# A hybrid decoder step on one core: where the last group's products stand among its slabs, and three small edits at the end of the second half

## The chip, the cores and the metric

The kernel runs on 1 core of one Trainium2 chip. The metric is the device time of one execution in microseconds, lower is better. Times of the kernel before: 1749.98, 1751.42 and 1751.07, median 1751.07. The engines are called as in the profile: PE (TensorE) multiplies matrices, DVE (VectorE), ACT (ScalarE) and POOL (GpSimd) work element by element, SP (SyncE) here only issues DMAs. ACT issues some DMAs too, and an engine that waits to issue one does nothing else meanwhile.

## The reference, cut to what matters

One layer for 256 prompt tokens and 8 x 8 sample tokens, 320 in all, with a model width of 2048. The change lies in the second half, the convolutional feed-forward network:

```python
def conv_ffn(h, conv_state, w_up, conv_w, conv_b, w_down):
    up = h @ w_up                                    # 2048 -> 2 * 5632
    up, new_conv = causal_depthwise_conv(up, conv_state, conv_w, conv_b)
    g, u = jnp.split(up, 2, axis=-1)
    return (jax.nn.gelu(g, approximate=True) * u) @ w_down, new_conv

def rms_norm(x, w):
    xf = x.astype(jnp.float32)
    y = xf * lax.rsqrt(jnp.mean(xf * xf, axis=-1, keepdims=True) + EPS)
    return (y * w.astype(jnp.float32)).astype(x.dtype)

    f, new_ffn_conv = conv_ffn(rms_norm(x, p["norm_ffn_pre"]), ffn_conv_state,
                               p["ffn_w_up"], p["ffn_conv_w"], p["ffn_conv_b"], p["ffn_w_down"])
    x = x + rms_norm(f, p["norm_ffn_post"])
```

## The kernel before

**Products in three matmuls.** Everything is float32. A weight or an activation is split into a rounded high part and a low part: for a slab of weights `wraw`, ACT casts `whi` (line 124) and DVE subtracts it to get `wlo` (line 125). A product is then three matmuls, high by high, high by low and low by high (lines 135 to 137 for the up-projection, line 1472 for the prompt tokens in the down-projection).

**Groups.** The 5632 hidden columns are cut into 11 groups of 512, numbered 0 to 10. `ffn_up(g)` makes the up-projection of a group: 16 slabs of 512 KB, 24 matmuls each, first the gate half, then the other half. DVE copies the result out of PSUM into `pad` (lines 1338, 1339), ACT and DVE do the convolution (`gcv`, `ucv`; lines 1345, 1347), ACT the GELU, and DVE multiplies into `a` and `a_s` for prompt and sample tokens (lines 1355, 1356). `cut` splits quarters of `a` into `a11`, `a12`, `a21`, `a22` (high parts on ACT, line 398, low parts on DVE, line 399).

**The down-projection one group behind.** While PE works on the slabs of group g, `down_steps` makes the down-projection of group g - 1. It does so for two halves of the output columns (m = 0, 1), each with seven products of half-sized blocks in place of eight, after Strassen and Winograd. Their weights are the four loaded blocks `b11`, `b12`, `b22`, `b21` and four combinations t1 to t4 that POOL makes from them (line 1513, each in four pieces); t3, t2 and t4 are written over the blocks b12, b11 and b21. The order of products in a half is 1 (b11), 2 (b21) with the sample tokens' products `pms` ahead of it, 5 (t1), 7 (t3), 3 (b22), 6 (t2), 4 (t4). For each, ACT and DVE split the weights (lines 1487, 1488), PE makes six matmuls into `pm`, and DVE adds `pm` to a sum (line 1466). `together(m)` then combines the seven sums of a half into blocks of the output with seven additions on DVE (line 1566).

**What sets the order.** `down_steps` is a generator. After each slab of an up-projection `tick` advances it by one step, so one product stands behind each slab. It first yields two or more times without work, and so starts that many slabs later. What is left after the last slab runs at once, without slabs between. A scheduler then orders each engine's instructions; an engine runs them in that order.

**The last group.** Group 10 has no group behind it whose slabs could hide its down-projection. `down_plain` makes it plainly, in eight steps of 256 x 512 weights (two row pairs i times four column blocks nb), called steps one to eight below. `held_w` (step two, and step four for the other row pair) and `kept` are weights that stay for a second use; step one is (nb 0, i 0), step two (nb 1, i 0), step three (nb 0, i 1), step four (nb 1, i 1), then the same for nb 2 and 3. Behind steps two, four, six and eight come the samples' products `pds`. Row pair i = 1 needs `a12` and `a22`. Tokens 128 to 255 (c = 1) are finished first, then the samples (c = 2), then tokens 0 to 127 (c = 0).

**The end.** For each finished block (c, nb), `one_block` sums the squares on ACT and multiplies the block by the norm's weights, in place; `whole(c, ...)` makes the inverse root of the mean square with a handful of one-column steps on DVE and ACT (`last_s`, `last_v`, `last_r`, `last_n`), adds the scaled blocks to `x1_tok` and stores them as y. For two blocks of c = 1 ACT scales and POOL adds (lines 1708, 1709), for the others DVE does both (line 1711).

**x1 in rows.** `to_rows`, four times in the first half of the products of group 0, turns x1 on DVE (line 1448) and stores it to memory from SP (line 1451); `load_x1` reads it again at the end as `x1_tok`.

Of the kernel before, what the change touches and what calls it, by code (L numbers as in the profile page):

```python
# [8 lines left out]
F32 = mybir.dt.float32  # L9
# [3 lines left out]
ALU = mybir.AluOpType  # L13
# [3 lines left out]
P = 128  # L17
# [16 lines left out]
def hybrid_step(  # L34
# [10 lines left out]
    act, dve, pool, pe, sp = nc.scalar, nc.vector, nc.gpsimd, nc.tensor, nc.sync  # L45
# [1261 lines left out]
    with tc.tile_pool(name="fp", bufs=1) as fp:  # L1307
# [92 lines left out]
        NG = NF // 4  # L1400
# [81 lines left out]
        def down_steps(ck, parts):  # L1482
# [9 lines left out]
            if ck == 0:  # L1492
                for _ in range(3):
                    yield
            else:
                for _ in range(5 if ck == NG - 2 else 2):
                    yield
            for m in (1, 0) if ck == 0 else (0, 1):
# [24 lines left out]
                product(1, "a11", "b11")  # L1523
                if ck == 0 and m == 1:
                    to_rows(0)
                yield
# [7 lines left out]
                if ck == 0 and m == 1:  # L1534
                    to_rows(1)
                yield
                raw["t3"] = raw["b12"]
                less(raw["t3"], "b22", "b12")
                product(5, "s1", "t1")
                yield  # L1540
                raw["t2"] = raw["b11"]
# [101 lines left out]
        gain_s = hp.tile([P, 1024], F32, tag="ohi", name="gain_s")  # L1643
        unread = hp.tile([P, 512], F32, tag="olo", name="unread")
        x1_tok = hp.tile([P, 5, 1024], F32, tag="h_lo", name="x1_tok").rearrange("p a b -> p (a b)")
# [26 lines left out]
        def one_block(c, nb):  # L1672
            t, g, _ = of(c, nb)
            by_vector = c == 0 and nb > 1
            with first() if by_vector else nullcontext():
                act.activation(unread, t, AF.Square, accum_out=squares[:, c, nb:nb + 1])
                (dve if by_vector else pool).tensor_tensor(out=t, in0=t, in1=g, op=ALU.mult)
                if c < 2 and nb == 2:
                    most[c] = fp.tile([P, 1], F32, name=f"most{c}")
                    dve.tensor_reduce(out=most[c], in_=squares[:, c, :3], axis=mybir.AxisListType.X, op=ALU.add)  # L1680
                    dve.tensor_scalar(out=most[c], in0=most[c], scalar1=1.0 / D, scalar2=EPS, op0=ALU.mult, op1=ALU.add)
# [13 lines left out]
        def whole(c, some, others):  # L1695
            with first():
# [7 lines left out]
                for nb in range(2 if c == 2 else 4):  # L1704
# [7 lines left out]
                    if c < 2:  # L1712
                        (act if by_two or c == 0 and nb % 2 else sp).dma_start(o_y[P * c:P * c + P, 512 * nb:512 * nb + 512], y)
                if c == 2:
# [96 lines left out]
```

## Time and profile before

| | |
|---|---|
| time of the profiled execution | 1750.16 us |
| its span, first to last instruction | 1748.4 us |
| median of three runs | 1751.07 us |
| PE busy | 1727.3 us, 99% |
| DVE busy | 1365.8 us, 78% |
| ACT busy | 880.1 us, 50% |
| POOL busy | 694.9 us, 40% |

A row of the timeline gives the start, the duration, the engine, the line, the operation, out<-in, the shape and a count; in brackets the idle time of the engine before it and what ended that. "<-DVE wlo L1488" means that DVE's instruction of line 1488, which writes `wlo`, ended the wait. A matmul row's duration is longer than the distance to the next one, since matmuls are pipelined; distances from start to start are the better measure.

### The profile page before, as it was taken

To read this page: it belongs to the slowest core of one execution; us is meant where nothing else is said; L and a number is where in the kernel's file an instruction comes from. 1 tells how busy PE (TensorE), PEld (TensorE's weight loads), DVE (VectorE), ACT (ScalarE), POOL (GpSimd) and SP (SyncE) were. 2 spreads that over 40 slices of the span, in tenths; PEclk is the share of its full clock that TensorE was granted. 3 is DMA by queue.
4 is the path that set the end of the run, shared out by engine and by line. 5 is a ranking of instruction groups with operands and counts; after the bars stand their busy time and mean duration, and the time that the engine had idled before them with its cause. 6 is when DMAs were issued, how large, how long until landed. Compare 5 with 4: busy or idle time off the path is not lost.

```text
span 1748.4 us, 29947 instructions
## 1 busy us (share of the span) xinstructions
PE 1727.3 (99%) x11223; PEld 1606.9 (92%) x11223; DVE 1365.8 (78%) x2133; ACT 880.1 (50%) x1274; POOL 694.9 (40%) x1003
## 2 busy tenths in 40 slices
PE   9999999999999999999999999999999999999987
PEld 9999999999999999999988888988888888888874
DVE  6559864667979787878987788879797979797897
ACT  6344544334656664645565444444444545454543
POOL 2532230000422323121355656565555556565463
PEclk9999999999999999999999999999999999999998
DMA  8776665555676776654765454454545454545353
GB/s 265 223 231 182 182 176 157 154 165 185 211 228 205 216 230 215 217 178 155 241 187 149 147 158 147 146 179 150 167 148 164 153 161 146 162 154 159 122 168 125
DMA packets 214482, 310.60 MB, mean 178 GB/s; under 512 B 22080, under 2 KB 115904, under 8 KB 214144
## 3 DMA queue, kind: packets, MB, share of 16 engines
q1 hardware_dynamic: 196800, 279.23, 52.4%
q0 software_dynamic: 6176, 13.87, 2.6%
q10 hardware_dynamic: 11360, 15.57, 2.6%
q8 instruction: 88, 1.44, 0.3%
q14 instruction: 58, 0.48, 0.1%
HBM read 285.00 MB, written 22.32 MB: 176 GB/s over the span
## 4 chain that ended last, share of the span: by engine, by line
PE 94%; DVE 3%; POOL 2%; issue 1%; ACT 0%; DVEq 0%; ACTq 0%; POOLq 0%
PE ps L135 20%; PE ps L137 20%; PE ps L136 20%; PE pm L1472 10%; PE pd L135 4%; PE pd L136 4%; PE pd L137 4%; PE pms L1479 3%; POOL b L1513 1%; PE pd L1472 1%; PE y_ps L1088 1%; PE ps_v L136 1%; PE ps_v L135 1%; PE ps_v L137 1%; DVE wlo L1488 1%
## 5 line engine op out<-in xcount | busy, mean ns | idle before, releaser
L137 PE MATMUL ps<-h_hi,wlo 128*128 128x320 f32 x2428 | 749.1, 309 | 1.4 <-DVE wlo L125 1.3
L135 PE MATMUL ps<-h_hi,whi 128*128 128x320 f32 x2428 | 750.1, 309 | 0.0
L136 PE MATMUL ps<-h_lo,whi 128*128 128x320 f32 x2428 | 748.6, 308 | 0.0
L125 DVE TENSOR_TENSOR wlo<-wraw,whi 128x1024 fp32r<-128x1024 f32 (+2 forms) x395 | 490.1, 1242 | 146.3 <-ACT whi L124 144.3
L124 ACT CAST whi<-wraw 128x1024 fp32r<-128x1024 f32 (+2 forms) x394 | 406.2, 1031 | 370.0 <-PE ps L136 142.1
L135 PEld LDWEIGHTS ps<-h_hi,whi 128*128 128x128 f32 x2428 | 455.7, 188 | 9.0 <-issue 1.3
L136 PEld LDWEIGHTS ps<-h_lo,whi 128*128 128x128 f32 x2428 | 455.8, 188 | 6.2
L137 PEld LDWEIGHTS ps<-h_hi,wlo 128*128 128x128 f32 x2428 | 455.5, 188 | 2.6 <-DVE wlo L125 2.6
L1488 DVE TENSOR_TENSOR wlo<-b,whi 128x1024 fp32r<-128x1024 f32 x120 | 154.0, 1284 | 77.2 <-ACT whi L1487 76.0
L1487 ACT CAST whi<-b 128x1024 fp32r<-128x1024 f32 x120 | 125.4, 1046 | 163.8 <-PE ps L136 147.0
L1513 POOL TENSOR_TENSOR b<-b,b 128x256 f32<-128x256 f32 x160 | 185.9, 1186 | 0.0
L135 PE MATMUL pd<-ohi,whi 128*128 128x320 f32 x448 | 138.7, 310 | 0.0
L137 PE MATMUL pd<-ohi,wlo 128*128 128x320 f32 x448 | 138.3, 309 | 0.0
L136 PE MATMUL pd<-olo,whi 128*128 128x320 f32 x448 | 138.3, 309 | 0.0
L1350 POOL COPY ptf<-pad 128x2 f32<-128x2 f32 x88 | 41.0, 465 | 177.7 <-DVE pad L1338 177.2
L1513 POOL TENSOR_TENSOR b<-b,t 128x256 f32<-128x256 f32 x80 | 78.6, 992 | 69.9 <-PE pms L1479 67.5
L1513 POOL TENSOR_TENSOR t<-b,b 128x256 f32<-128x256 f32 x80 | 90.4, 1159 | 26.6 <-DMA b<-in_ffn_w_down 26.5
L135 PEld LDWEIGHTS pd<-ohi,whi 128*128 128x128 f32 x448 | 84.1, 188 | 0.6
L136 PEld LDWEIGHTS pd<-olo,whi 128*128 128x128 f32 x448 | 84.1, 188 | 0.3
L137 PEld LDWEIGHTS pd<-ohi,wlo 128*128 128x128 f32 x448 | 84.1, 188 | 0.0
L248 DVE TENSOR_TENSOR acc_mix<-acc_mix,pd 128x320 f32<-128x320 f32 (+1 forms) x113 | 53.5, 477 | 27.6 <-PE pd L137 27.5
L1479 PE MATMUL pms<-b,a_s 128*64 128x512 f32 x320 | 74.1, 599 | 0.0
(417 smaller groups left out, 2498.2 us busy)
## 6 DMA issues: line engine op xcount, KB each, us to landing
wraw<-in_ffn_w_up SPq DMA_DIRECT2D x176, 512.0 KB, 4.6
wraw<-in_w_in SPq DMA_DIRECT2D x132, 512.0 KB, 3.8
b<-in_ffn_w_down SPq DMA_DIRECT2D x80, 512.0 KB, 4.6
wraw<-in_w_out SPq DMA_DIRECT2D x64, 512.0 KB, 3.5
st<-in_state_ssm SPq DMA_DIRECT2D x40, 256.0 KB, 4.5
out_ssm_state_sample<-st ACTq DMA_DIRECT2D x30, 256.0 KB, 2.4
cs<-dacs_d SPq DMA_DIRECT2D x16, 320.0 KB, 5.5
wraw<-in_w_in SPq DMA_DIRECT2D x12, 384.0 KB, 4.1
```

The costliest lines, as they stand in the source:

```text
L124: rounded[:] = [act.copy(hi, raw).ins]
L125: lowered[:] = [dve.tensor_tensor(out=lo, in0=raw, in1=hi.bitcast(F32), op=ALU.subtract).ins]
L135: pe.matmul(ps, whi, xhi, start=first, stop=False)
L136: pe.matmul(ps, whi, xlo, start=False, stop=False)
L137: last_made[0] = pe.matmul(ps, wlo, xhi, start=False, stop=last).ins
L248: added_last[:] = [dve.tensor_tensor(out=acc[:, nb, ts], in0=acc[:, nb, ts], in1=ps[:, ts], op=ALU.add).ins]
L1350: kept_rows[:] = [pool.tensor_copy(ptf[:, k, :], pad[:, 256:258]).ins]
L1472: last_made[0] = pe.matmul(ps, x[xi][:, k], w[wi][:, 512 * k:512 * k + 512], start=start and k + i == 0, stop=stop and k == 1 and i == 2).ins
L1479: last_made[0] = pe.matmul(ps[64 * h:64 * h + 64], a_s[:, k0 + k], w[h][:, 512 * k:512 * k + 512], start=start and k == 0, stop=stop and k ...
L1487: rounded[:] = [act.copy(hi, raw).ins]
L1488: dve.tensor_tensor(out=lo, in0=raw, in1=hi.bitcast(F32), op=ALU.subtract)
L1513: pool.tensor_tensor(out=to[:, cs], in0=raw[x][:, cs], in1=raw[y][:, cs], op=ALU.subtract)
```

## The change

Five edits in the second half:

1. For the last group that has steps (`ck == NG - 2`, group 9, whose products run among group 10's slabs) `down_steps` yields two times without work and not five.
2. Two of the stores of y for c = 1, those of the blocks that POOL adds, are issued by SP and not by ACT.
3. Block (0, 1) is multiplied by the norm's weights on DVE and not on POOL.
4. Block (0, 3), the last, is multiplied into a room of its own (`scaled_last`, the second half of the tile that held `unread`) and not in place.
5. The first two turns of x1 are called one product later each.

```diff
@@ down_steps
-                for _ in range(5 if ck == NG - 2 else 2):
+                for _ in range(2):
                     yield
@@
                 product(1, "a11", "b11")
-                if ck == 0 and m == 1:
-                    to_rows(0)
                 yield
@@
                 product(2, "a12", "b21")
                 if ck == 0 and m == 1:
-                    to_rows(1)
+                    to_rows(0)
                 yield
                 raw["t3"] = raw["b12"]
                 less(raw["t3"], "b22", "b12")
                 product(5, "s1", "t1")
+                if ck == 0 and m == 1:
+                    to_rows(1)
                 yield
@@
-        unread = hp.tile([P, 512], F32, tag="olo", name="unread")
+        spare = hp.tile([P, 2, 512], F32, tag="olo", name="unread")
+        unread, scaled_last = spare[:, 0], spare[:, 1]
@@ one_block
-            by_vector = c == 0 and nb > 1
+            by_vector = c == 0 and nb > 0
             with first() if by_vector else nullcontext():
                 act.activation(unread, t, AF.Square, accum_out=squares[:, c, nb:nb + 1])
-                (dve if by_vector else pool).tensor_tensor(out=t, in0=t, in1=g, op=ALU.mult)
+                if (c, nb) == (0, 3):
+                    f[0][3] = scaled_last
+                (dve if by_vector else pool).tensor_tensor(out=f[0][3] if (c, nb) == (0, 3) else t, in0=t, in1=g, op=ALU.mult)
@@ whole
-                        (act if by_two or c == 0 and nb % 2 else sp).dma_start(o_y[P * c:P * c + P, 512 * nb:512 * nb + 512], y)
+                        (act if c == 0 and nb % 2 else sp).dma_start(o_y[P * c:P * c + P, 512 * nb:512 * nb + 512], y)
```

What this does to the order on the engines is shown at three places. The first is ACT at the end of group 10's slabs. A cast of line 1487 belongs to a product of the seven, a cast of line 124 from `wraw` to a slab of the up-projection or to a step of the last down-projection, one from `raw` to such a step; line 398 cuts the quarters of `a`. Before:

```order
L1487 CAST whi<-t_18393 128x1024
L124 CAST whi<-wraw 128x1024
L1487 CAST whi<-b_18345 128x1024
L1487 CAST whi<-b_18347 128x1024
L398 CAST a_hi<-a 128x256
L1487 CAST whi<-b_18343 128x1024
L1345 ACTIVATE ucv<-pad,prm 128x336 x2
L1487 CAST whi<-b_18349 128x1024
L124 CAST whi<-wraw 128x1024
L124 CAST held_w<-wraw 128x1024
L124 CAST whi<-wraw 128x1024
L398 CAST a_hi<-a 128x256
```

And now, from the last two products on:

```order
L1487 CAST whi<-b_18217 128x1024
L124 CAST whi<-wraw 128x1024
L1487 CAST whi<-b_18223 128x1024
L124 CAST whi<-wraw 128x1024
L1345 ACTIVATE ucv<-pad,prm 128x336
L124 CAST held_w<-wraw 128x1024
L1345 ACTIVATE ucv<-pad,prm 128x336
L124 CAST whi<-wraw 128x1024
L124 CAST held_w<-raw 128x1024
L124 CAST whi<-raw 128x1024 x2
L398 CAST a_hi<-a 128x256 x2
```

Before, the casts for products 7, 3, 6 and 4 followed the last slab's; now only that of product 4 does, and the last two quarters `a12`, `a22` are cast behind two more casts, those from `raw` for steps five and six.

The second place is DVE at the same time, where the low parts of the weights are made. Before, from the first sum behind the last slab's convolution:

```order
L1466 TENSOR_TENSOR in_fp_10060<-in_fp_10060,pm_18556 128x512
L399 TENSOR_TENSOR a12_lo_18523<-a_17739,a12_hi_18522 128x256
L1466 TENSOR_TENSOR in_fp_10060<-in_fp_10060,pm_18568 128x512
L1488 TENSOR_TENSOR wlo_18577<-b21_18349,whi_18576 128x1024
L125 TENSOR_TENSOR wlo_18599<-wraw_18597,whi_18598 128x1024
L125 TENSOR_TENSOR held_w_18588<-wraw_18617,held_w_18588 128x1024
```

And now (the rows from the first `ucv` step to the split of step three; ahead of them stand the split of product 4, the sum of product 6, the split of step one, two pairs of `pad` copies and one addition of line 1566):

```order
L1347 SCALAR_TENSOR_TENSOR ucv_18533<-pad_18528,prm_96,ucv_18533 128x336
L1566 TENSOR_TENSOR in_fp_10060<-in_fp_10060 128x512
L1347 SCALAR_TENSOR_TENSOR ucv_18533<-pad_18528,prm_96,ucv_18533 128x336
L1347 SCALAR_TENSOR_TENSOR ucv_18558<-pad_18553,prm_96,ucv_18558 128x336
L1355 TENSOR_TENSOR a_17739<-ucv_18533,gcv_17738 128x256
L1356 TENSOR_TENSOR a_s_17740<-ucv_18533,gcv_17738 128x64
L1347 SCALAR_TENSOR_TENSOR ucv_18558<-pad_18553,prm_96,ucv_18558 128x336
L1466 TENSOR_TENSOR in_fp_10060<-in_fp_10060,pm_18578 128x512
L1355 TENSOR_TENSOR a_17739<-ucv_18558,gcv_17738 128x256
L1356 TENSOR_TENSOR a_s_17740<-ucv_18558,gcv_17738 128x64
L125 TENSOR_TENSOR held_w_18588<-wraw_18617,held_w_18588 128x1024
L125 TENSOR_TENSOR wlo_18634<-wraw_18632,whi_18633 128x1024
```

The split of product 4 (line 1488, from b21) stood behind the convolution of the last slab and now stands ahead of it; the split of `held_w`, which step two needs, still stands behind it.

The third place is DVE near the end, between the sums of blocks (0, 1) and (0, 2), `pd_1_0` and `pd_2_0`. Before:

```order
L1466 TENSOR_TENSOR in_mix_10462<-in_mix_10462,pd_1_0_18784 128x512
L1699 TENSOR_SCALAR last_v2_18809<-both_halves_18807,eps_9645 128x1
L1700 RECIPROCAL last_v2_18809<-last_v2_18809 128x1
L1701 TENSOR_TENSOR last_r2_18811<-last_s2_18810,last_v2_18809 128x1
L1702 SCALAR_TENSOR_TENSOR last_n2_18812<-last_s2_18810,last_r2_18811 128x1
L1703 SCALAR_TENSOR_TENSOR last_r2_18811<-last_n2_18812,last_r2_18811 128x1
L1711 SCALAR_TENSOR_TENSOR x1_tok_18591<-in_mix_10462,last_r2_18811,x1_tok_18591 128x512
L1466 TENSOR_TENSOR in_fp_10060<-in_fp_10060,pd_2_0_18800 128x512
```

And now:

```order
L1466 TENSOR_TENSOR in_mix_10462<-in_mix_10462,pd_1_0_18784 128x512
L1680 TENSOR_TENSOR in_mix_10462<-in_mix_10462,gain_13410 128x512
L1702 TENSOR_SCALAR last_v2_18809<-both_halves_18807,eps_9645 128x1
L1703 RECIPROCAL last_v2_18809<-last_v2_18809 128x1
L1704 TENSOR_TENSOR last_r2_18811<-last_s2_18810,last_v2_18809 128x1
L1705 SCALAR_TENSOR_TENSOR last_n2_18812<-last_s2_18810,last_r2_18811 128x1
L1466 TENSOR_TENSOR in_fp_10060<-in_fp_10060,pd_2_0_18800 128x512
L1706 SCALAR_TENSOR_TENSOR last_r2_18811<-last_n2_18812,last_r2_18811 128x1
L1714 SCALAR_TENSOR_TENSOR x1_tok_18591<-in_mix_10462,last_r2_18811,x1_tok_18591 128x512
```

The multiplication of block (0, 1) has come from POOL and stands ahead of the samples' inverse root; the rest keeps its order. Of the x1 turns (edit 5) no row moves: DVE's turns and SP's stores stand between the same neighbours, and up to group 10 the order of all five engines is the same in both kernels.

## The prediction

> **What bounds the kernel now.** I read the page's span and chain first, then who makes PE wait, then the stretches, then PE's rows around the longest wait.
>
> ```profile
> span 1748.4 us, 29947 instructions
> PE 94%; DVE 3%; POOL 2%; issue 1%; ACT 0%; DVEq 0%; ACTq 0%; POOLq 0%
> ...
> PE pm L1472 <- DVE wlo L1488: 5.1, 3, 4.1
> ...
> 1532.00:1612.00 80.00, 80.00 (x480) 70.88 (x479) 66.69 (x95) 39.12 (x49) 43.65 (x63) 1.00 0.49 151
> 1692.00:1704.00 12.00, 7.93 (x34) 6.30 (x33) 12.00 (x21) 7.38 (x10) 4.27 (x6) 0.92 0.86 258
> ```
>
> The chain is PE for 94%, so time is PE's work plus PE's holes plus what follows PE. The columns of the stretches are the length, then PE, PEld, DVE, ACT, POOL busy, then the granted clock. Group 9 (1532 to 1612) has no hole. The end of group 10 (1692 to 1704) has PE at 7.93 of 12 us, DVE busy throughout, clock 0.92. From 1600 us on the row of waits counts three on this split, 5.1 us in all, the longest 4.1.
>
> ```profile
> 1701.91 0.71 PE L1472 MATMUL pm<-wlo,a_hi 128*128 128x512 f32 x1 [4.07 <-DVE wlo L1488]
> ...
> 1703.69 0.63 PE L1472 MATMUL pd<-whi,a_hi 128*128 128x512 f32 x1
> ...
> 1705.66 0.40 PE L1472 MATMUL pd<-wlo,a_hi 128*128 128x512 f32 x1
> ...
> 1689.25 5.03 POOL L1513 TENSOR_TENSOR b<-b,b 128x256 f32<-128x256 f32 x4
> 1695.31 1.03 ACT L1487 CAST whi<-b 128x1024 fp32r<-128x1024 f32 x1
> 1700.65 1.21 DVE L1488 TENSOR_TENSOR wlo<-b,whi 128x1024 fp32r<-128x1024 f32 x1
> ```
>
> PE stands before the third matmul of the last product (number 4). Its weights are t4, which POOL finishes at 1694.28; ACT casts them from 1695.31, and DVE, still on the convolution of the last slab, splits them only at 1700.65. Before, four products follow the last slab, so POOL's and DVE's work for them meets the convolution.
>
> **The change, part by part.** *Products three ticks earlier.* The number of instructions is unchanged. Group 10 takes group 9's rhythm: first product behind the third slab, last behind the sixteenth.
>
> ```profile
> 1528.53 0.31 PE L135 MATMUL ps<-h_hi,whi 128*128 128x320 f32 x1
> ...
> 1611.85 0.31 PE L135 MATMUL ps<-h_hi,whi 128*128 128x320 f32 x1
> ```
>
> Group 9 runs from its first slab's matmul, 1528.53, to the next group's, 1611.85: 83.32 us. Group 10 ran from 1611.85 to its first `pd` matmul, 1703.69: 91.84. If it goes as group 9 did, it gains **8.52 us**. The five intervals from 1703.69 to 1705.66 took 1.97 us, against 5 x 0.23 at full clock (six matmuls in 1.39 us, next rows): without the long hole another **0.80** comes back.
>
> What is late next is the second step of the last down projection, whose matmuls need DVE's split of `held_w`.
>
> ```profile
> 1688.11 0.39 PE L1472 MATMUL pm<-whi,s_hi 128*128 128x512 f32 x1
> ...
> 1689.50 0.31 PE L135 MATMUL ps<-h_hi,whi 128*128 128x320 f32 x1
> ...
> 1693.02 0.39 PE L1472 MATMUL pm<-whi,s_hi 128*128 128x512 f32 x1
> ...
> 1695.66 1.99 DVE L1347 SCALAR_TENSOR_TENSOR ucv<-pad,prm,ucv 128x336 f32<-128x336 f32 x4
> 1697.58 0.41 DVE L1355 TENSOR_TENSOR a<-ucv,gcv 128x256 f32<-128x256 f32 x1
> ...
> 1698.05 0.67 DVE L1466 TENSOR_TENSOR in_fp<-in_fp,pm 128x512 f32<-128x512 f32 x1
> 1698.64 0.41 DVE L1355 TENSOR_TENSOR a<-ucv,gcv 128x256 f32<-128x256 f32 x1
> ...
> 1701.78 1.21 DVE L125 TENSOR_TENSOR wlo<-wraw,whi 128x1024 fp32r<-128x1024 f32 x1
> ...
> 1713.19 0.69 DVE L1566 TENSOR_TENSOR in_fp<-in_fp 128x512 f32<-128x512 f32 x1
> ```
>
> From start to start a product is 1.39 us and a slab 3.52; on DVE a split is 1.13, a sum taken in 0.59, four `ucv` steps 1.92, a pair `a` and `a_s` 0.47; a pair of `pad` copies, of the same 256 and 64 columns, I take as 0.47 too, and an add of L1566, as long as a sum taken in, as 0.60. Count from the end of product 6 in the second half. PE then does slab 16, product 4, the twelve matmuls of step one and two of step two: 3.52 + 1.39 + 2.78 + 0.46 = 8.15. DVE's split for product 4 ends about 0.8 after the same point (ACT's cast starts when slab 15 is done, 1.39 before it, then 1.03 and 1.13). Then the built order gives: two sums taken in (1.18), the split of step one (1.13), two `pad` pairs (0.94), two adds (1.20), four `ucv` (1.92), two `a` pairs (0.94), the split of `held_w` (1.13): 8.44, so it ends at 9.2. PE waits 1.1, with the hand-over **1.2 us**. A wait this short I cost without a clock loss. The trace has one other wait of this length:
>
> ```profile
> 890.71 0.41 PE L137 MATMUL ps<-h_hi,wlo 128*128 128x320 f32 x1 [1.04 <-DVE wlo L125]
> 890.96 0.31 PE L135 MATMUL ps<-h_hi,whi 128*128 128x320 f32 x1
> ```
>
> Behind it matmuls took 0.31 us, as at 1528.53; behind 4.07 they took 0.63 and not 0.40. Ends: 0, if DVE has 1.2 us to spare, and 2.8, if the clock falls too.
>
> *POOL's subtractions* now press on product 7 of the second half, whose weights are t3.
>
> ```profile
> 1583.53 1.62 POOL L1513 TENSOR_TENSOR b<-b,t 128x256 f32<-128x256 f32 x1 [3.55 <-PE pms L1479]
> ...
> 1587.88 2.43 POOL L1513 TENSOR_TENSOR b<-b,b 128x256 f32<-128x256 f32 x2
> ...
> 1595.74 0.39 PE L1472 MATMUL pm<-whi,s_hi 128*128 128x512 f32 x1
> ...
> 1675.44 8.22 POOL L1513 TENSOR_TENSOR b<-b,t 128x256 f32<-128x256 f32 x2 [2.40 <-DVE wlo L1488]
> ...
> 1675.50:1683.00 7.50, 7.50 (x38) 4.39 (x37) 7.50 (x10) 2.41 (x3) 7.50 (x2) 1.00 0.48 142
> ```
>
> In group 9 t3 was done at 1590.3 and product 7 began at 1595.74; its third matmul, 0.46 later, is the first that needs the low part: 5.9 us. Behind t3 in the new order stand a cast (1.03), ACT's and DVE's `ucv` steps (0.6 and 0.5) and the split (1.13): 3.3, with hand-overs 3.5. So POOL may be 2.4 us later than in group 9 before PE waits. DVE is fuller here, with the adds of the first half's sums between the splits, and POOL has two subtractions in the trace that took 8.22 us, in a stretch (the last row, columns as above) in which DVE was busy for all 7.5 us. I take **0.4 us** of waiting; the ends are 0 and 3.4, below as a rival.
>
> *Tail: the store queue, the multiplication moved to VectorE, the room of the last block.*
>
> ```profile
> 1731.75 0.67 DVE L1466 TENSOR_TENSOR in_mix<-in_mix,pd 128x512 f32<-128x512 f32 x1
> 1733.70 0.22 DVE L1699 TENSOR_SCALAR last_v<-both_halves,eps 128x1 f32<-128x1 f32 x1 [1.27 <-ACT last_s L1698]
> ...
> 1734.54 1.15 DVE L1703 SCALAR_TENSOR_TENSOR last_r<-last_n,last_r 128x1 f32<-128x1 f32 x1
> ...
> 1738.60 0.68 DVE L1466 TENSOR_TENSOR in_fp<-in_fp,pd 128x512 f32<-128x512 f32 x1
> ...
> 1740.12 0.69 DVE L1677 TENSOR_TENSOR in_fp<-in_fp,gain 128x512 f32<-128x512 f32 x1 [0.79 <-ACT unread L1676]
> ...
> 1741.82 1.41 DVE L1711 SCALAR_TENSOR_TENSOR x_tok<-in_mix,last_r,x_tok 128x512 f32<-128x512 f32 x2
> ...
> 1733.40 0.26 ACT L1698 ACTIVATE last_s<-both_halves,eps 128x1 f32<-128x1 f32 x1 [3.81 <-POOL x_tok L1709]
> ...
> 1734.36 1.32 POOL L1677 TENSOR_TENSOR in_mix<-in_mix,gain 128x512 f32<-128x512 f32 x1 [1.37 <-ACT unread L1676]
> ...
> 1735.12 0.39 PE L1472 MATMUL pd<-kept,a_hi 128*128 128x512 f32 x1
> ```
>
> ACT stood 3.81 us at two stores that wait for POOL, with the samples' root behind them; DVE waited 1.27 for that root, and one of its one-column steps took 1.15 while POOL multiplied. Both go. In return DVE must now wait for ACT's square and multiply. Before, block (0,1)'s sum at 1731.75 to block (0,3)'s at 1738.60 is 6.85. Now: from sum to multiplication 1.52 (as from 1738.60 to 1740.12), the multiplication 0.61, four one-column steps 0.84, a sum 0.60, one step 0.19, two `x_tok` 1.34, a multiplication 0.61 and a reduction 0.07: 5.78. PE, done soon after 1735.12, still comes first. From 1738.60 to the first output at 1741.82 were 3.22; the last multiplication now runs beside ACT's square: 0.61 less. Together **1.7 us**. SP, which takes the two stores, next has the samples' stores, due behind the step at 1734.54, and ACT's wait shows POOL done by 1733.40; so they cost nothing, and if POOL came later, the samples' stores would be late by as much, still ahead of the last ones. Ends: 0 and 2.4 (both removed waits, 1.27 and about 1.0, gone with nothing given back, and rounding).
>
> *x1 turned one product later.* In the built order DVE's turns and SP's stores of them stand where they stood, on every engine: 0.
>
> **Sum.** 8.5 + 0.8 - 1.2 - 0.4 + 1.7 = 9.4 us less. The profiled execution took 1750.16 us, which gives 1740.8; it lies 0.9 below the median of 1751.07, which would give 1741.7. I say 1741.2.
>
> **The rivals.**
>
> *POOL is starved.* If DVE holds POOL off as at 1675.44, two subtractions take 8.2 us and not the 2.4 of group 9: t3 comes 5.8 late, of which 2.4 are free. That is 3.4 of waiting and about 1.6 of slow clock (0.8 on the product and 0.8 behind it, as after the 4.07). 9.4 + 0.4 - 5.0 = 4.8: 1745.4. For it: the 8.22 us. Against: group 9, and DVE's pauses in the new order, where it waits for PE's sample products. The Trainium skill, "SBUF — State Buffer", section "SBUF: two separate sides", says that a VectorE instruction with two SBUF inputs and a GpSimd instruction that reads SBUF exclude each other for one whole instruction. By that rule a subtraction would lose at most the 1.2 us of one split and the sum would stay as above; here two lost 5.8 us, more than one instruction each, so the trace does not bear out that limit.
>
> *The tail gives nothing back*, because DVE, which now does POOL's multiplication, is what sets it: 7.7 us in all, 1742.5. For it: DVE is in nearly every row of the last chain.
>
> *Slower: the last `a` halves stuck behind a load on ACT.* In the new order ACT casts `a12_hi` behind the weights of steps five and six; those of step five are loaded only after product 4's split.
>
> ```profile
> x_tok<-x_rows SPq DMA_DIRECT2D x4, 512.0 KB, 6.8
> raw<-in_ffn_w_down SPq DMA_DIRECT2D x3, 512.0 KB, 4.6
> ```
>
> PE needs `a12_hi` at 8.15 + 1.2 + four matmuls 0.93 + the sample products 1.87 = 12.2 after product 6; ACT needs two casts and a third, 2.4, and the load starts at 0.8: it may take 9.0 us. Such loads took 4.6, and the slowest group beside them 6.8. Each us beyond is one of PE's, and 1.6 of clock behind a long one; slower by over 0.2% from about 20 us on: 1754.
>
> *It does not do what it says*: the hole only moves behind the last slab, as deep as before, 1750.
>
> **How the numbers follow.** Forecast 0.62, starved POOL 0.16, no tail 0.10, hole only moved 0.07, slower 0.05. The low end is no new wait at all, 11.0 less, with half the spread of the runs: 1738.5. The high end is the starved POOL, 1745.4, with the 1.6 of a clock loss on `held_w`: 1747.0. A measurement here tells about 0.2%, 3.5 us, from no change; the first three cases lie beyond: faster 0.88, same 0.07, slower 0.05.
>
> **What would show it.** Right: no PE wait on L1488 in group 10's end and its stretch at the 83 us of group 9; one wait of about 1.2 us on `held_w` at the second step; no slow clock behind it; ACT's root of the samples free of POOL, no 1.15 us step on DVE, the last multiplication beginning before the square ends. Wrong: PE waits at product 7 on a split behind POOL; PE waits at `a12`; or the end after PE's last matmul as long as before.

## The result, and the profile after

| | before | changed |
|---|---|---|
| median, six runs each in turn on one chip | 1750.77 us (1749.92 to 1751.42) | 1744.79 us (1743.87 to 1745.46) |
| profiled execution | 1750.16 us, span 1748.4 | 1744.75 us, span 1743.0 |
| group 10, first slab to first `pd` matmul | 91.84 us | 86.90 us |
| from there to the end of PE's last matmul | 31.82 us | 32.55 us |
| from there to the end of the span | 12.89 us | 11.07 us |

The ratio is 0.9966, with a 95% interval of 0.9953 to 0.9979: the changed kernel is faster by 6.0 us, by the interval 3.7 to 8.2. The forecast was 9.4 us less. The time lies inside the forecast's range, the sign is right, and a third of the gain is missing.

The two profiles differ by 5.4 us and not 6.0, since group 10 began at 1611.85 before and at 1612.48 now. These 0.63 us are already there in the first ten microseconds, at the first loads. In the fourteen profiles of this study group 10 begins between 1611.2 and 1612.8, whatever the edits. So profiles are compared here from the start of group 10 to the end of the span: 136.55 us before and 130.52 now, 6.03 less, which agrees with the medians.

First the page of the changed kernel, its span and its chain by engine:

```profile
span 1743.0 us, 29949 instructions
...
PE 93%; DVE 5%; issue 1%; POOL 0%; ACT 0%; DMA 0%; SPq 0%; DVEq 0%; ACTq 0%; POOLq 0%
```

POOL, 2% of the chain before, is gone from it, and DVE has risen from 3% to 5%. The waits of PE from 1610 us on, in the changed kernel (total, number, longest, in us):

```profile
PE pm L1472 <- DVE wlo L1488: 1.9, 1, 1.9
PE pd L1472 <- DVE held_w L125: 1.3, 1, 1.3
PE ps L137 <- DVE wlo L125: 0.8, 1, 0.8
```

The hole of 4.07 us is gone. In its place stand three shorter ones, each on a split that DVE makes. Group 10's boundaries on PE in the changed kernel, and the wait on `held_w`:

```profile
1612.48 0.31 PE L135 MATMUL ps<-h_hi,whi 128*128 128x320 f32 x1
...
1699.38 0.40 PE L1472 MATMUL pd<-whi,a_hi 128*128 128x512 f32 x1
...
1704.08 0.74 PE L1472 MATMUL pd<-held_w,a_hi 128*128 128x512 f32 x2 [1.27 <-DVE held_w L125]
```

Compared slab by slab and product by product with group 9 of the same execution (83.32 us), group 10 is longer at three places and nowhere else: its sixth slab takes 4.54 us and not 3.52, product 7 of the second half 3.53 and not 1.38, and slab 14 3.92 and not 3.52. That is 1.02 + 2.15 + 0.40 = 3.57, and 83.32 + 3.57 = 86.89.

The end, in the changed kernel, on PE, DVE and ACT:

```profile
1731.54 0.39 PE L1472 MATMUL pd<-kept,a_hi 128*128 128x512 f32 x1
...
1728.18 0.68 DVE L1466 TENSOR_TENSOR in_mix<-in_mix,pd 128x512 f32<-128x512 f32 x1
...
1733.81 0.68 DVE L1466 TENSOR_TENSOR in_fp<-in_fp,pd 128x512 f32<-128x512 f32 x1
...
1734.52 0.69 DVE L1680 TENSOR_TENSOR unread<-in_fp,gain 128x512 f32<-128x512 f32 x1
...
1736.43 1.42 DVE L1714 SCALAR_TENSOR_TENSOR x_tok<-in_mix,last_r,x_tok 128x512 f32<-128x512 f32 x2
...
1729.58 0.24 ACT L1701 ACTIVATE last_s<-both_halves,eps 128x1 f32<-128x1 f32 x1
...
1734.58 0.63 ACT L1677 ACTIVATE unread<-in_fp 128x512 f32<-128x512 f32 x1 [2.06 <-DVE most L1684]
```

From block (0,1)'s sum to block (0,3)'s are 5.63 us (6.85 before), from there to the first output 2.62 (3.22 before). The samples' root follows ACT's square with no wait on POOL, and the last multiplication begins (1734.52) before ACT's square does (1734.58).

**What DVE had to do.** The stretches of group 9 and of group 10 in the changed kernel (length, then PE, PEld, DVE, ACT, POOL busy, clock, DMA):

```profile
1529.20:1612.50 83.30, 83.30 (x502) 74.19 (x501) 70.00 (x98) 39.98 (x50) 47.21 (x65) 1.00 0.49 153
1612.50:1699.40 86.90, 84.14 (x502) 74.16 (x501) 81.48 (x115) 42.46 (x55) 47.59 (x61) 1.00 0.46 142
```

DVE is busy for 70.0 us in group 9 and for 81.5 in group 10. Of the 11.5 us more, ten additions of L1566 are 7.3 us and three more `ucv` steps, with longer rows for some of the eleven, 2.6. Forecast was a group 10 of 83.7 us: DVE would have had to be busy for 97% of it, in an order in which one late instruction holds up all behind it. The load is not even. Of the 86.9 us DVE is idle for 5.4, but between slabs 11 and 15 (1666.6 to 1688.8) only for 0.35 of 22.2.

The first wait shows how little it takes. DVE from the sum of product 2 on and POOL beside it, in group 9 (traced in the kernel before) and then in group 10 of the changed kernel, and PE's slab 6 there:

```profile
1552.12 0.67 DVE L1466 TENSOR_TENSOR in_mix<-in_mix,pm 128x512 f32<-128x512 f32 x1
1552.72 1.26 DVE L125 TENSOR_TENSOR wlo<-wraw,whi 128x1024 fp32r<-128x1024 f32 x1
...
1552.85 5.84 POOL L1513 TENSOR_TENSOR b<-b,b 128x256 f32<-128x256 f32 x4
```

```profile
1636.10 0.67 DVE L1466 TENSOR_TENSOR in_mix<-in_mix,pm 128x512 f32<-128x512 f32 x1
1636.81 0.69 DVE L1566 TENSOR_TENSOR in_mix<-in_mix 128x512 f32<-128x512 f32 x1
1637.42 1.76 DVE L125 TENSOR_TENSOR wlo<-wraw,whi 128x1024 fp32r<-128x1024 f32 x1
...
1636.83 6.36 POOL L1513 TENSOR_TENSOR b<-b,b 128x256 f32<-128x256 f32 x4
...
1639.23 0.41 PE L137 MATMUL ps<-h_hi,wlo 128*128 128x320 f32 x1 [0.75 <-DVE wlo L125]
```

One addition of `together` stands ahead of the slab's split, and the split itself takes 1.76 us and not 1.26. POOL subtracts beside both. In group 9 the split began 0.13 us before POOL's next piece, and that piece took 1.73 us; in group 10 a piece (1636.83 to 1638.10) was already under way. The second wait, at product 7 (POOL, ACT, DVE, then PE, in the changed kernel):

```profile
1674.26 2.94 POOL L1513 TENSOR_TENSOR b<-b,b 128x256 f32<-128x256 f32 x2
1677.16 0.73 POOL L1513 TENSOR_TENSOR b<-b,t 128x256 f32<-128x256 f32 x1
1677.86 3.61 POOL L1513 TENSOR_TENSOR b<-b,b 128x256 f32<-128x256 f32 x4
...
1677.68 1.04 ACT L1487 CAST whi<-b 128x1024 fp32r<-128x1024 f32 x1
...
1677.80 2.13 DVE L1347 SCALAR_TENSOR_TENSOR ucv<-pad,prm,ucv 128x336 f32<-128x336 f32 x2 [0.27 <-ACT ucv L1345]
1679.86 0.68 DVE L1466 TENSOR_TENSOR in_fp<-in_fp,pm 128x512 f32<-128x512 f32 x1
1680.46 0.41 DVE L1355 TENSOR_TENSOR a<-ucv,gcv 128x256 f32<-128x256 f32 x1
1680.79 0.76 DVE L1356 TENSOR_TENSOR a_s<-ucv,gcv 128x64 f32<-128x64 f32 x1
1681.48 0.55 DVE L1347 SCALAR_TENSOR_TENSOR ucv<-pad,prm,ucv 128x336 f32<-128x336 f32 x1
1681.95 1.21 DVE L1488 TENSOR_TENSOR wlo<-b,whi 128x1024 fp32r<-128x1024 f32 x1
...
1683.22 0.50 PE L1472 MATMUL pm<-wlo,s_hi 128*128 128x512 f32 x1 [1.87 <-DVE wlo L1488]
```

POOL has t3 ready at 1677.2 and ACT has it cast at 1678.7, in time for PE, which could use the low part from 1681.2 on. But DVE is in the convolution of group 10's own second half, of which two column blocks of four are projected first, so that their convolution falls between slabs 12 and 14. In group 9 all four come behind the last slab, and at this point DVE, in the kernel before, was idle for 2.29 us:

```profile
1592.01 1.49 DVE L1488 TENSOR_TENSOR wlo<-b,whi 128x1024 fp32r<-128x1024 f32 x1 [2.29 <-ACT whi L1487]
```

So three theories were to be told apart: DVE's order, POOL's stretching of DVE's instructions (they take longer while POOL works beside them), and the forecast's rival, t3 late on POOL.

### The profile page after: what moved, and what is told of

Same layout as the page of the kernel before. It is cut to its first block, busy times and chain, and to the rows that moved or that the text cites. A ratio compares the mean times of both kernels' runs of the same rounds, so it can differ in the third digit from the quotient of the medians.

```text
span 1743.0 us, 29949 instructions
## 1 busy us (share of the span) xinstructions
PE 1725.0 (99%) x11223; PEld 1606.3 (92%) x11223; DVE 1370.3 (79%) x2134; ACT 880.6 (51%) x1274; POOL 692.3 (40%) x1002
## 4 chain that ended last, share of the span: by engine, by line
PE 93%; DVE 5%; issue 1%; POOL 0%; ACT 0%; DMA 0%; SPq 0%; DVEq 0%; ACTq 0%; POOLq 0%
PE ps L135 19%; PE ps L137 19%; PE ps L136 19%; PE pm L1472 10%; PE pd L135 4%; PE pd L137 4%; PE pd L136 4%; PE pms L1479 3%; DVE wlo L125 1%; PE y_ps L1088 1%; PE ps_v L136 1%; PE ps_v L135 1%; PE ps_v L137 1%; DVE wlo L1488 1%; PE pd L1472 1%
## 5 line engine op out<-in xcount | busy, mean ns | idle before, releaser
L1488 DVE TENSOR_TENSOR wlo<-b,whi 128x1024 fp32r<-128x1024 f32 x120 | 153.9, 1283 | 73.3 <-ACT whi L1487 73.0
L1513 POOL TENSOR_TENSOR b<-b,t 128x256 f32<-128x256 f32 x80 | 71.9, 908 | 78.7 <-PE pms L1479 78.7
```

Of the source, the lines that this page charges most:

```text
L1488: dve.tensor_tensor(out=lo, in0=raw, in1=hi.bitcast(F32), op=ALU.subtract)
L1513: pool.tensor_tensor(out=to[:, cs], in0=raw[x][:, cs], in1=raw[y][:, cs], op=ALU.subtract)
```

## The experiments

e1 to e4 and e7 to e9 start from the changed kernel, the others from the kernel before. In the table "end" is the time from the end of PE's last matmul to that of the span, and "from group 10 on" the time from that group's start to the span's end, all from one profiled execution, so a difference of some tenths there is not told from chance. The ratios are to the kernel before, run on the same chip between them.

| | group 10 | end | from group 10 on | median, us | ratio and interval |
|---|---|---|---|---|---|
| before | 91.84 | 12.89 | 136.55 | 1750.77 | |
| changed | 86.90 | 11.07 | 130.52 | 1744.79 | 0.9966 (0.9953 to 0.9979) |
| e1 t3 first | 86.82 | 11.27 | 130.64 | 1744.95 | 0.9970 (0.9958 to 0.9982) |
| e2 additions held | 86.35 | 11.50 | 131.51 | 1746.97 | 0.9979 (0.9969 to 0.9988) |
| e3 t4 held | 86.16 | 11.12 | 129.82 | 1744.34 | 0.9965 (0.9952 to 0.9978) |
| e4 one width | 85.39 | 11.16 | 133.36 | 1745.86 | 0.9976 (0.9967 to 0.9986) |
| e5 first edit alone | 86.81 | 12.92 | 132.27 | 1747.02 | 0.9984 (0.9975 to 0.9993) |
| e6 end alone | 91.04 | 11.08 | 134.04 | 1748.08 | 0.9989 (0.9980 to 0.9998) |
| e7 convolution later | 85.73 | 11.65 | 130.28 | 1743.34 | 0.9961 (0.9949 to 0.9974) |
| e8 e7 and additions | 84.99 | 11.17 | 132.63 | 1745.97 | 0.9977 (0.9968 to 0.9986) |
| e9 three loosenings | 85.53 | 11.67 | 130.12 | 1743.84 | 0.9962 (0.9949 to 0.9976) |

**e1: t3 ahead of t2 on POOL.**

```diff
 def less(to, x, y):
-    with tc.high_priority(offset=100000), tc.issue_after(last_rows):
+    with tc.high_priority(offset=100000), tc.issue_after(last_less[0] if (ck, m) == (NG - 2, 1) else last_rows):
...
-        pool.tensor_tensor(out=to[:, cs], ...)
+        last_less[0] = pool.tensor_tensor(out=to[:, cs], ...).ins
```

> The changed kernel, but POOL makes all four pieces of t3 before the four of t2 in the second half of group 9's columns, so t3 is ready about 3 us earlier (four pieces of about 1.2 us instead of seven). The order on DVE and ACT is the same. Theory 'late t3' (the rival of the prediction: PE waits at product 7 because POOL delivers t3 late): the wait of 1.87 us before product 7's third matmul goes, group 10 takes 86.90 - 2.15 - 0.40 = 84.4 us, the kernel is 2.5 us faster than the changed one (about 1742.3). Theory 'DVE's queue' (t3 and its cast are in time, the split stands behind two conv steps, a sum and the a pair in DVE's order): the wait stays within 0.5 us of 1.87 and group 10 near 86.9 us, about 1744.8.

POOL, ACT and DVE in e1 around product 7:

```profile
1667.74 5.07 POOL L1513 TENSOR_TENSOR b<-b,b 128x256 f32<-128x256 f32 x4 [7.04 <-PE pms L1479]
...
1676.89 1.03 ACT L1487 CAST whi<-b 128x1024 fp32r<-128x1024 f32 x1
...
1681.15 1.21 DVE L1488 TENSOR_TENSOR wlo<-b,whi 128x1024 fp32r<-128x1024 f32 x1
```

t3 is ready at 1672.8, some 3.7 us earlier when the two starts of group 10 are set equal, and nothing follows from it: ACT and DVE keep their order, the wait is 1.78 us and group 10 86.82. That POOL delivers t3 late is not the cause.

**e2: the additions of `together` behind their half's last sum.**

```diff
-    product(4, "a22", "t4")
+    last_sum[m] = product(4, "a22", "t4")
...
 def plus(x, y, op=ALU.add):
-    dve.tensor_tensor(out=t[x], in0=t[y], in1=t[x], op=op)
+    with tc.issue_after(last_sum[m]):
+        dve.tensor_tensor(out=t[x], in0=t[y], in1=t[x], op=op)
```

> The changed kernel, but each of the fourteen additions of together() must stand behind the last sum of its half on DVE, so that none stands ahead of a split that PE needs: the one at 1636.81, ahead of slab 6's split, the one at 1674.23, ahead of slab 13's, and the two among the conv steps before held_w's split go elsewhere; the scheduler also puts product 7's split ahead of the a pair and of the third ucv step. Theory 'DVE's queue': slab 6 takes 3.52 and not 4.54 us, product 7's wait is under 0.5 us, the wait on held_w under 0.3 us; group 10 takes 83.3 to 83.9 us, and the kernel is 4 to 5 us faster than the changed one (1740 to 1741). Theory 'late t3': slab 6 and held_w as said, but product 7's wait stays near 1.9 and group 10 near 85.9 us; about 1742.5. Theory 'the adds are filler that costs nothing': no change, 1744.8.

PE's waits from 1610 us on in e2:

```profile
PE ps L137 <- DVE wlo L125: 2.2, 1, 2.2
PE both_halves L1695 <- DVE most L1690: 2.0, 1, 2.0
PE pm L1472 <- DVE wlo L1488: 0.3, 1, 0.3
```

Slab 6 takes 3.51 us, as expected, and the wait on `held_w` is gone: the addition ahead of the split and the two ahead of `held_w`'s account for these two waits. Product 7 waits 0.26, but slab 14, next on DVE, now waits 2.21. Six additions of the second half run near the end, two one-column steps there take 0.94 and 1.23 us beside POOL, and PE's sum for the samples is 2.05 late. The expected 1740 to 1741 did not come. The place of the additions alone does not explain the loss.

**e3: t4 only behind the split of t3.**

```diff
...
-    raw["t4"] = raw["b21"]
-    less(raw["t4"], "t2", "b21")
+    raw["t4"], late = raw["b21"], (ck, m) == (NG - 2, 1) and pool.tensor_copy(fp.tile([P, 1], F32, name="late"), parts_of[1][:, 1023:].bitcast(F32)).ins
+    less(raw["t4"], "t2", "b21", late)
```

`late` is a one-column copy of the split of t3 on POOL; `less` now issues t4 behind it.

> The changed kernel, but POOL begins t4 in the second half of group 9's columns only when DVE has split t3 (a one-column copy of the split's result on POOL stands in front). In the changed kernel t4's pieces ran at 1677.9 to 1681.5, beside the ucv steps that took 2.13 us for two (1.0 elsewhere) and an a_s step that took 0.76 (0.21 elsewhere). Theory 'POOL stretches DVE': without t4 beside them these give back about 1.7 us, product 7's wait falls from 1.87 to 0.2 to 0.6 us and group 10 from 86.90 to about 85.3 us; slab 6's wait of 0.75 stays. Theory 'late t3' and theory 'DVE's order alone': the wait stays near 1.9 and group 10 near 86.9 us.

DVE in e3, the two `ucv` steps and the split of t3, and PE two slabs later:

```profile
1678.03 1.19 DVE L1347 SCALAR_TENSOR_TENSOR ucv<-pad,prm,ucv 128x336 f32<-128x336 f32 x2 [0.28 <-ACT ucv L1345]
...
1680.68 1.22 DVE L1488 TENSOR_TENSOR wlo<-b,whi 128x1024 fp32r<-128x1024 f32 x1
...
1689.29 0.41 PE L137 MATMUL ps<-h_hi,wlo 128*128 128x320 f32 x1 [0.54 <-DVE wlo L125]
```

With the same order on DVE and without t4 beside them the two steps take 1.19 us and not 2.13, and product 7's wait falls from 1.87 to 0.33, as the theory of POOL's stretching said. The t4 pieces now run beside later splits, slab 15 waits 0.54 for one, and slab 14 takes 3.92 us as before: of the 1.5 us won at product 7, 0.7 is left in group 10, which takes 86.16 us and not the expected 85.3.

**e4: group 10's second half projected in one go.**

```diff
-    if g < NG - 1:
+    if g < NG:
         project(ffn_w_up, DFF + 512 * g, lambda j, ps: evac(1, j, ps))
```

> The changed kernel, but group 10's second half is projected in one go of 512 columns, as in the groups before, and not in two of 256, so no convolution falls between slabs 12 and 16 and all four fall behind the last slab. Theory 'DVE's queue': product 7's wait goes, as it was 0 in group 9, and slab 14 takes 3.52 us; slab 6's 0.75 stays; but the four convolutions and the cuts of a then stand before the last down projection, and PE waits several us there (3 to 8), so the kernel is slower than the changed one by 1 to 6 us. Theory 'late t3': product 7's wait stays near 1.9 us, as t3 comes as late as before.

DVE's split of t3 in e4, which now waits for ACT's cast, and PE in step one of the last down-projection:

```profile
1678.23 1.37 DVE L1488 TENSOR_TENSOR wlo<-b,whi 128x1024 fp32r<-128x1024 f32 x1 [1.71 <-ACT whi L1487]
...
1701.77 0.80 PE L1472 MATMUL pd<-wlo,a_hi 128*128 128x512 f32 x1 [2.88 <-DVE wlo L125]
```

Product 7 takes 1.39 us and slab 14 3.52, as in group 9: the convolution in the middle of the second half is what DVE was behind with. Slab 6 keeps its 0.74. The convolution is now due behind the last slab, and PE waits 2.88 us there, with a slow clock behind it: 2.8 us worse from group 10 on, and 1.1 us in the medians (the profiled execution is the second longest of ten). POOL has t3 ready as late as in the changed kernel, 64.7 us after the start of group 10. The theory of DVE's queue gave both, the one of a late t3 neither.

**e5 and e6: the parts alone.** e5 is the kernel before with two yields in place of five, e6 the kernel before with edits 2, 3 and 4.

```diff
-                for _ in range(5 if ck == NG - 2 else 2):
+                for _ in range(2):
```

> The kernel before with the first edit alone (two yields in place of five); the four other edits are left out. If the parts add up and the x1 turns are worth nothing: group 10 takes 86.9 us, with the waits of the changed kernel (0.75 at slab 6, 1.9 at product 7, 1.3 on held_w), and the end behind PE's last matmul stays at 12.9 us: 1746.5 us, 4.2 less than before. If instead the end is hidden or changed by the earlier products: 1744.8.

> The kernel before with edits 2, 3 and 4 alone (the two stores on SP, block (0,1) multiplied on DVE, the last block's own room); the five yields and the x1 turns stay. If the parts add up: group 10 takes 91.8 us with the 4.07 us hole, and the end behind PE's last matmul 11.1 us in place of 12.9: 1749.0 us, 1.8 less than before. If the tail's gain needs the earlier products: 1750.7.

e5 has the changed kernel's group 10 (86.81) and the old end (12.92), e6 the new end (11.08) and the old hole. In medians of runs taken together (before 1750.08) they gain 3.1 and 2.0 us, together 5.1, with intervals of about 1.6 us to each side; the whole change gained 6.0. For e5 4.2 were expected; its profiled execution, the fastest of eleven, gained 4.3. So the parts add up as far as this can be measured, and the x1 turns, which are in neither, need no share.

**e7: the convolution of the first two column blocks without the highest priority.**

```diff
-    with first() if g == NG - 1 and half == 1 else nullcontext():
+    with first() if g == NG - 1 and half == 1 and j > 1 else nullcontext():
```

> The changed kernel, but the convolution of group 10's first two column blocks of the second half no longer has the highest priority; so DVE has the splits of product 7 and of slab 14 ahead of the first a pair and the last two ucv steps, with the same work in all. Theory 'DVE's order' (the splits stand behind convolution that nobody needs yet): product 7's wait falls from 1.87 to about 0.5, slab 14 takes 3.5 to 3.6 and not 3.92 us, group 10 about 84.9 us: 2.0 us faster than the changed kernel, 1742.8. Theory 'DVE is too full there' (as the held additions and the held t4 only moved the wait to slabs 14 and 15): the waits move on to product 3 or slab 15 and less than 0.8 us is gained: 1744 or more.

DVE in e7, the split of t3 and two one-column steps of the end, and POOL beside the latter:

```profile
1681.20 1.21 DVE L1488 TENSOR_TENSOR wlo<-b,whi 128x1024 fp32r<-128x1024 f32 x1
...
1722.72 0.93 DVE L1704 TENSOR_TENSOR last_r<-last_s,last_v 128x1 f32<-128x1 f32 x1
1723.69 1.25 DVE L1705 SCALAR_TENSOR_TENSOR last_n<-last_s,last_r 128x1 f32<-128x1 f32 x1
...
1721.10 2.54 POOL L1680 TENSOR_TENSOR in_fp<-in_fp,gain 128x512 f32<-128x512 f32 x2 [2.77 <-ACT unread L1677]
1723.64 1.28 POOL L1680 TENSOR_TENSOR in_fp<-in_fp,gain_s 128x512 f32<-128x512 f32 x1
```

Product 7 waits 1.09 and not the expected 0.5, since the two stretched `ucv` steps and a sum still stand ahead of the split; slab 14 takes 3.52. Group 10 gains 1.17 us, between what the two theories said. Behind it most is lost again, 0.35 up to PE's last matmul and 0.58 at the end, where DVE's one-column steps (0.40 and 0.16 us in the changed kernel) now meet POOL's multiplications.

**e8: e7, the first half's additions behind its last sum, the second half's at once behind `held_w`'s split.**

```diff
+                    with tc.issue_after(behind[m]), tc.high_priority(offset=100000 * m):
...
+                        held_split[:] = held_split or lowered if n == 1 else held_split
...
+                            behind[1] = held_split[0]
                             together(1)
```

> The kernel of e7 and, in addition, the additions of the first half stand behind its last sum, and those of the second half behind held_w's split but with a priority that puts them there at once and not at the end as in e2. If DVE's queue is the cause of all three waits: slab 6 takes 3.52 us, product 7 waits at most 0.5, held_w at most 0.3, and the samples' root is not late as it was in e2 (2.05 us there): group 10 takes 83.4 to 84.0 us and the kernel 1740 to 1741, 4 to 5 us less than the changed one. If the additions are late at the end again: about 1742.5.

DVE in e8 behind the additions, and PE's wait for it:

```profile
1710.97 3.42 DVE L125 TENSOR_TENSOR wlo<-raw,whi 128x1024 fp32r<-128x1024 f32 x2
...
1713.31 0.50 PE L1472 MATMUL pd<-wlo,a_hi 128*128 128x512 f32 x1 [3.33 <-DVE wlo L125]
```

Group 10 is shorter by 1.9 us, with no wait at slab 6 or on `held_w`; product 7 waits 0.88, more than the 0.5 that were expected at most. The seven additions then run from 1703.4 on, ahead of the splits of steps five and six, and PE waits 3.33 us for the first of these. Neither number came: the median is 1745.97, some 5 us above the one and 3.5 above the rival's 1742.5. The additions did cost PE a wait, but at another place than the rival said.

**e9: three loosenings together**: e7, t4 held as in e3, and the additions of the first half alone held as in e2.

> The changed kernel with the three loosenings that helped alone: the additions of the first half stand behind its last sum (slab 6), the convolution of group 10's first two column blocks loses its highest priority (e7), and t4 begins behind the split of t3 (e3). The additions of the second half stay as in the changed kernel, so held_w's wait of 1.27 stays. Theory 'DVE is full and POOL stretches it': slab 6 takes 3.52 us, product 7 waits 0 to 0.3, slab 15 may wait up to 0.8 us as in e3; group 10 takes 83.4 to 84.4 us and the kernel 2.5 to 3.5 us less than the changed one, 1741.3 to 1742.3. If the same work only moves the wait again, as in e2 and e8: group 10 over 85.5 us and 1743.5 or more.

PE's waits from 1610 us on in e9:

```profile
PE pd L1472 <- DVE held_w L125: 1.6, 1, 1.6
PE pm L1472 <- DVE wlo L1488: 0.8, 2, 0.6
PE ps L137 <- DVE wlo L125: 0.2, 1, 0.2
```

Slab 6 takes 3.52 us and product 7 waits 0.16, but product 3 waits 0.59, two slabs are 0.4 and 0.5 us longer, and `held_w`'s wait is 0.3 longer. Group 10 takes 85.53 us, where 83.4 to 84.4 were expected from three gains that had each been seen before; the rival, over 85.5 us and 1743.5 or more, is what came. From group 10 on it gains 0.4 us on the changed kernel. Its ratio and that of e7 can't be told from the changed kernel's: neither is shown to be faster.

**e10, e11, e12: edits 2, 3 and 4 alone**, each on the kernel before and with one profiled execution (edit 4 with the lines of `one_block` that use the new room).

```diff
-    (act if by_two or c == 0 and nb % 2 else sp).dma_start(...)
+    (act if c == 0 and nb % 2 else sp).dma_start(...)
...
-    by_vector = c == 0 and nb > 1
+    by_vector = c == 0 and nb > 0
...
-    unread = hp.tile([P, 512], F32, tag="olo", name="unread")
+    spare = hp.tile([P, 2, 512], F32, tag="olo", name="unread")
+    unread, scaled_last = spare[:, 0], spare[:, 1]
```

> The kernel before with edit 2 alone: the two stores of y of the blocks that POOL adds are issued by SP. The end behind PE's last matmul was 12.89 us before and 11.07 with edits 2 to 4. If the stores on ACT hold up the samples' root and that is what is late: the end is 11.9 to 12.1 us, and DVE's wait of 1.27 us for the root goes. If the samples' root is not what the end waits for: 12.9.

> The kernel before with edit 3 alone: block (0,1) is multiplied by the norm's weights on DVE and not on POOL. If POOL's multiplication beside DVE costs what the one-column step of 1.15 us showed, but DVE pays for the multiplication itself (0.61): the end behind PE's last matmul is 12.6 to 12.9 us. If the waiting stores on ACT remain the cause: 12.9 to 13.5, since DVE has more to do and the root comes as late.

> The kernel before with edit 4 alone: the last block's multiplication by the norm's weights goes into a room of its own and need not wait for ACT's square. If that is worth the length of the multiplication, which then runs beside the square: the end behind PE's last matmul is 12.2 to 12.4 us in place of 12.89. If the root, not the product, is what the last step waits for: 12.9.

The ends behind PE's last matmul are 12.48, 12.60 and 12.33 us, against 12.89: 0.41, 0.29 and 0.56 less, 1.26 in all, where the three together give 1.82. The four times are of single executions. e10 kept DVE's wait for the samples' root at 1.00 us, since the root then stands behind ACT's square, and POOL's multiplication still stretched a one-column step to 0.77: without the one the other edit is worth less. That miss is of 0.4 us; e11 and e12 came as expected.

## Why the prediction was right, and where it was not

**Products three ticks earlier: the mechanism right, the size not.** The term was 8.5 us, from the step "If it goes as group 9 did", less 0.4 for POOL. Group 10 gained 4.94. This is nearly the whole of the error: 83.7 was forecast, 86.90 came, 3.2 of the 3.4 us that are missing. The step that failed is the one that took group 9's rhythm over by PE's matmuls alone and never summed DVE's work in the stretch. The rows were there: in the kernel before, DVE's 1532 to 1612 stood at 66.69 of 80 us, and its group 10 was, as a window of the same trace shows, as heavy as now:

```profile
1612.00:1703.70 91.70, 86.41 (x502) 74.48 (x501) 81.02 (x122) 44.58 (x58) 50.94 (x61) 0.99 0.49 148
```

These 81 us, part of them DVE's own lengthening beside POOL, did not fit into 83.3 in any order that was run, with PE waiting for single instructions of them. What the forecast put ahead of the split of t3 was one ACT and one DVE step of the convolution, 0.6 and 0.5; in the trace it was 4.2 us: two steps that took 2.13 together, a sum, the `a` pair and a third step. So of the prediction's signs of being right the 83 us of group 10 did not come, and PE did wait at product 7 on a split of L1488.

**POOL's subtractions.** t3 came 2.0 us later than in group 9 (8.8 us from the first of POOL's pieces there and not 6.8), within the 2.4 that were counted as free, and e1 shows that even an early t3 changes nothing. So the rival "POOL is starved" has the right place, product 7, and nearly the right time, 1745.4, by a mechanism that the runs refute. The measured 1744.79 lies nearer to it than to the forecast's 1741.2, and inside a range whose upper end was built on this rival; that the range held there is luck. What e3 shows is the other direction: POOL stretches DVE. In group 10 the prediction looked only at what DVE does to POOL.

**The 0.80 behind the long hole, and the 1.2 on `held_w`: right.** Between the first `pd` matmul and the last PE took 0.73 us more, which is 1.53 for `held_w`'s step (3.04 us, against 1.51 in e2, where it does not wait) less 0.80. The wait itself is 1.27 us. The count of instructions there was therefore good, and no slow clock followed, as was said.

**The end: right.** 1.7 was said and 1.82 measured; the two parts, 5.78 and 2.61, came as 5.63 and 2.62. Of the mechanism the singles show one thing that the prediction did not say: the three edits are worth some 0.5 us more together than one by one, as far as single executions show it.

**x1 turns: 0**, as said; the order up to group 10 did not change, and the sum of the parts, 5.1 of 6.0 us, needs nothing from them within its intervals.

**The other rivals.** PE nowhere waits for `a12` in the changed kernel, so the load on ACT's queue was early enough. The hole did not move behind the last slab; it did break up into three waits. The end gave 1.82 us, so the rival of a tail that gives nothing is out.

What stays open: how much the 81 us on DVE could be shortened, and whether an order of the same work exists that reaches 84 us. e7, e8 and e9 are three orders, of which the best takes 84.99. The account that DVE is too full rests on these runs and on the sum of its work; no run gave any of it to another engine.

## What to carry to other kernels

Before a stretch is forecast by the rhythm of its neighbour, add up what each engine has to do in it, not only the one that waits: an engine that would be busy for 97% of the forecast length is a rival bound, and none of the orders run here kept PE from waiting for it. A wait that one loosening removes at such an engine can come back at a later instruction of its queue, so gains seen singly need not add up (e9: slab 6's 1.0 from e2, e7's 1.2 and e3's 0.7 us in group 10, 1.4 together). And an engine off the path can lengthen another's instructions by working beside it: read the durations of the same instruction with and without company.

## What the runs showed of the hardware

**POOL and DVE lengthen each other's instructions.** A split of 128x1024 took 1.21 us alone and 1.76 beside POOL, an `a_s` step 0.21 and 0.76, a one-column step of the end 0.16 and 1.25 beside a multiplication of 128x512 on POOL. The sums of L1466, which have one input in PSUM, took 0.67 or 0.68 in either company. The Trainium skill, "SBUF — State Buffer", section "SBUF: two separate sides", says that the lock concerns a VectorE operation with two SBUF inputs against a GpSimd operation that reads SBUF, and holds for the whole instruction; these rows agree with both: the split of 1.76 us (1637.42) ends 1.08 us after POOL's piece that was under way, and e3 shows what it costs in time. The other way round POOL can lose more than one instruction's length: in the kernel before, a subtraction that takes 0.74 us elsewhere took 5.64 from 1678.02 on, while DVE ran two splits and four additions one behind the other.

**The clock behind a hole.** Behind PE's waits of 0.75, 1.27, 1.87 and 2.21 us matmuls went on at their old distances, after one longer step at most. Behind those of 2.9 to 4.1 us a row of matmuls took 0.63 and not 0.40 us, 0.43 and not 0.23 from start to start; in e8 the row began only 1 us after the wait's end. The number of these rows did not follow the hole: 10 in e4 behind 2.88, 5 in e8 behind 3.33 ahead of the samples' matmuls, 7 in e6 and 12 in e11 behind 3.8, and 5 and 6 behind 4.1 (e10, e12). So the 0.80 of the forecast, six such rows, is one draw; in e11 the same spell was twice as long, and that is why its time from group 10 on (137.22) lies above that of the kernel before. The Trainium skill, "TensorE: Matmul & The Clock Gate", section "Part 1: The HAM clock gate", says that the clock is halved after an idle window of about 3.4 us, released after as long a busy one, and that these windows run freely. The varying count of slow matmuls agrees with a window that runs freely. The limit is not tested sharply here: the waits of up to 2.21 us agree with it, and the 2.88 in e4 don't stand alone, since PE had begun only two matmuls in the 4.5 us before, with a wait of 0.58 ahead of them.
